# Reordering the projections, chains, first loads and output norm of a hybrid decoder layer

## The chip, the cores and the metric

The kernel runs on one core of one Trainium2 chip. The core has five engines with a queue of instructions each: TensorE (PE, matrix products), VectorE (DVE), ScalarE (ACT), GpSimd (POOL) and SyncE (SP, here used to issue DMAs). Each works through its queue in order, and semaphores tie them together. The metric is the time of one execution on the device in microseconds (us), lower is better; of several runs the median is taken.

## The reference

One decoder layer on 256 tokens of width 2048, all in float32:

```
u = rmsnorm(x, norm_mix_w)
q_a, k_a, v_a, z_a, beta_a, dec_a, q_b, k_b, v_b, gate_a, gate_b = split(u @ w_in)
y_a = gated_deltanet(...)      # causal conv of 4 taps + silu, l2 norm of q and k, chunked delta rule
                               # (a triangular solve per chunk), then rmsnorm(o) * silu(z_a)
y_b = moba_attention(...)      # 8 heads of 128, rmsnorm of q and k, relative bias, softmax
mix = sigmoid(gate_a) * (y_a @ w_branch_gdn) + sigmoid(gate_b) * (y_b @ w_branch_moba)
h   = x + mix @ w_out
u   = rmsnorm(h, norm_ffn_w)
out = h + (silu(u @ w_ffn_gate) * (u @ w_ffn_up)) @ w_ffn_down
```

The two branches have 8 heads of 128 each; the feed-forward width is 5632. With 256 tokens the attention has one block, so each query attends to its own past only.

## The kernel before

**Matrix products.** Each float32 product is made of three (or, where one matmul covers two, fewer instructions) products of rounded parts: a weight unit of 128 x 1024 values is loaded (`wraw`, seven buffers, issued by SP), ACT rounds it to `whi`, DVE subtracts to get `wlo` (L64, L65, four buffers each), and PE multiplies both with the upper and lower part of the activations. `Weights.get(u)` issues loads six units ahead and splits three units ahead. There are 504 units, in the order in which the jobs take them.

**Jobs.** `fm_jobs` (L143) makes a result with channels on partitions: per unit 8 pairs of a 512-wide (L156) and a 256-wide matmul (L157). `tm_job` (L165) makes one with tokens on partitions: per unit 12 matmuls of 512 (L177 to L179). The convolution's q, k, v projections are fm jobs of 4 units; z, attention's q, k, v, the gates, the branches and all later products are tm jobs.

**Chains.** The small work (norms, DeltaNet, attention) is written as Python generators in the list `chains`. `tick()` is called after every second unit (TICK): it first runs what is in `late` (convolution taps; `turn`, the transposes of a result), then one step, a hop, of the first chain. The framework's scheduler then puts each engine's instructions in order, by program order and by when it expects their inputs.

**Order of the work.** Group 0's convolution jobs (x is scaled and split beside the first two), beta and decay, z of group 0, then group 1's convolution jobs with `gdn(0)` running in the ticks beside them, z of group 1, attention's projections of both groups with the chains behind, gate and branch jobs of the first branch (`yaT`), of the second (`ybT`), w_out, feed-forward, down projection. A convolution job is evicted by ACT and DVE (L262, L263), scaled (L340), gets six taps of DVE (L348) and a silu (L350, L351).

**Inside `gdn`.** Decay matrices (L396 to L400, the subtraction on POOL), transposes and squares for the norms of q and k (L410, L412), the scaled products (`decayed`, L428), a pass through DRAM for the 16 x 16 blocks (`dm`, `lb`, L451 to L454), fifteen dependent steps of DVE (L470, L471), the solve of the two token halves, one after the other, each in one hop (L496 to L546), and `solve`, `attend` and `finish`. `finish` squares on ACT, takes a reciprocal root by twelve small DVE operations (`rsqrt`), multiplies twice on POOL (L569, L570), and transposes into yaT (L574).

**Inside `moba`.** Norm of q and k, transposes (L643), then per pair of heads the load of the bias (L653, SP), scores (L658 to L660), softmax (L662 to L673) and the product with v (L681 to L688).

**First loads.** SP loads `wmix` and W0 in two halves, then W1 to W6; ACT queues all of x's transposed chunks (L199, L202). `x_part` (L211) splits the unit first, then makes four pieces of aT, upper part on ACT (L215), lower on DVE (L216).

## Time and profile before

| | us |
|---|---|
| median of 3 runs (1499.58 to 1500.82) | 1499.75 |
| the profiled execution | 1498.37 |
| its span, first to last instruction | 1496.6 |
| PE busy | 1474.1 (98%) |
| DVE busy | 868.9 (58%) |
| ACT busy | 675.8 (45%) |
| POOL busy | 56.7 (4%) |

Busy time is the union of an engine's instructions. Matmuls are pipelined, so one that takes 390 ns from start to end is followed by the next after some 225 ns; the distance between starts tells the rate. An engine's idle time is put down to the instruction that released it. The granted TensorE clock is shown as 1.00 over the whole span.

### The profile page before, as it was taken

Reading aid. Unit: us, or ns where it says so; the run is one execution under the profiler, and the core shown is the slowest. Engines: PE = TensorE matmul, PEld = TensorE weight load, DVE = VectorE, ACT = ScalarE, POOL = GpSimd, SP = SyncE. Lnnn points to the kernel's source line nnn. Section 1 sums busy time; section 2 is a strip of 40 time slices with the busy share of each in tenths; the row PEclk is TensorE's granted clock in tenths of the full one; section 3 lists DMA queues with packets and bytes.
Section 4 is the critical chain, followed back from the end, with each engine's and each line's share of the span. In section 5 each row is a group of like instructions: output and inputs, shape, how many; then the busy total and the mean of one; then the engine's idle time right before and its main releaser. Section 6 shows DMA issues by size and latency. Waiting matters only on the chain.

```text
span 1496.6 us, 18724 instructions
## 1 busy us (share of the span) xinstructions
PE 1474.1 (98%) x7164; PEld 1227.0 (82%) x7164; DVE 868.9 (58%) x1161; ACT 675.8 (45%) x956; POOL 56.7 (4%) x48
## 2 busy tenths in 40 slices
PE   7999999999999999999999999999999999999998
PEld 6888778887878888888888888888888888888887
DVE  5978957866664445555565555555555555444443
ACT  6645445445454444444554444444444444333332
POOL 0003002301100000000000000000000000000000
PEclk9999999999999999999999999999999999999999
DMA  9564744753546666667666666666666566666661
GB/s 372 168 189 127 209 124 142 191 177 115 181 127 199 195 195 184 187 193 241 192 184 186 194 186 194 184 192 187 196 185 193 186 186 194 194 206 207 194 210 58
DMA packets 77450, 277.82 MB, mean 186 GB/s; under 512 B 8752, under 2 KB 9392, under 8 KB 76976
## 3 DMA queue, kind: packets, MB, share of 16 engines
q1 hardware_dynamic: 75456, 270.46, 59.7%
q10 hardware_dynamic: 1424, 4.59, 1.2%
q0 software_dynamic: 480, 1.57, 0.3%
q8 instruction: 56, 0.92, 0.3%
q14 instruction: 34, 0.28, 0.1%
HBM read 274.36 MB, written 2.23 MB: 185 GB/s over the span
## 4 chain that ended last, share of the span: by engine, by line
PE 91%; DVE 4%; DMA 2%; ACT 1%; issue 1%; POOL 0%; SPq 0%; DVEq 0%; ACTq 0%; POOLq 0%
PE ps L179 27%; PE ps L177 27%; PE ps L178 27%; PE ps L156 3%; PE ps L157 2%; PE pT L189 1%; DVE wlo L65 1%; DMA lb<-dm 1%; DMA bias<-in_relt 1%; DVE cacc L348 1%; DMA wraw<-in_w 0%; ACT whi L64 0%; PE pU L551 0%; PE pO L559 0%; PE pb L279 0%
## 5 line engine op out<-in xcount | busy, mean ns | idle before, releaser
L65 DVE TENSOR_TENSOR wlo<-wraw,whi 128x1024 fp32r<-128x1024 f32 (+1 forms) x505 | 619.9, 1229 | 521.7 <-ACT whi L64 519.7
L64 ACT CAST whi<-wraw 128x1024 fp32r<-128x1024 f32 (+1 forms) x505 | 530.0, 1051 | 680.2 <-PE ps L179 608.0
L177 PE MATMUL ps<-whi,uT 128*128 128x512 f32 x704 | 274.8, 390 | 0.0
L179 PE MATMUL ps<-whi,uT 128*128 128x512 f32 x704 | 273.9, 389 | 0.0
L178 PE MATMUL ps<-wlo,uT 128*128 128x512 f32 x704 | 273.9, 389 | 0.0
L177 PE MATMUL ps<-whi,aT 128*128 128x512 f32 x512 | 202.8, 396 | 0.0
L179 PE MATMUL ps<-whi,aT 128*128 128x512 f32 x512 | 201.3, 393 | 0.0
L178 PE MATMUL ps<-wlo,aT 128*128 128x512 f32 x512 | 200.4, 391 | 0.0
L179 PEld LDWEIGHTS ps<-whi,uT 128*128 128x128 f32 x704 | 132.2, 188 | 27.5
L177 PEld LDWEIGHTS ps<-whi,uT 128*128 128x128 f32 x704 | 132.2, 188 | 27.0
L178 PEld LDWEIGHTS ps<-wlo,uT 128*128 128x128 f32 x704 | 132.2, 188 | 27.0
L156 PE MATMUL ps<-aT,whi 128*128 128x512 f32 x384 | 137.6, 401 | 10.3 <-DVE aT L216 10.2
L179 PEld LDWEIGHTS ps<-whi,aT 128*128 128x128 f32 x512 | 96.2, 188 | 19.7
L177 PE MATMUL ps<-whi,high 128*128 128x512 f32 x288 | 112.0, 389 | 0.0
L178 PE MATMUL ps<-wlo,high 128*128 128x512 f32 x288 | 112.0, 389 | 0.0
L179 PE MATMUL ps<-whi,high 128*128 128x512 f32 x288 | 112.0, 389 | 0.0
L157 PE MATMUL ps<-aT,wlo 128*128 128x256 f32 x384 | 108.6, 283 | 3.1 <-DVE wlo L65 3.1
L178 PEld LDWEIGHTS ps<-wlo,aT 128*128 128x128 f32 x512 | 96.3, 188 | 18.7
L177 PEld LDWEIGHTS ps<-whi,aT 128*128 128x128 f32 x512 | 96.3, 188 | 18.4
L156 PEld LDWEIGHTS ps<-aT,whi 128*128 128x128 f32 x384 | 73.0, 190 | 27.4 <-DVE aT L216 10.2
L157 PEld LDWEIGHTS ps<-aT,wlo 128*128 128x128 f32 x384 | 73.4, 191 | 4.1 <-DVE wlo L65 4.0
L178 PEld LDWEIGHTS ps<-wlo,high 128*128 128x128 f32 x288 | 54.1, 188 | 11.3
(327 smaller groups left out, 1394.3 us busy)
## 6 DMA issues: line engine op xcount, KB each, us to landing
wraw<-in_w SPq DMA_DIRECT2D x503, 512.0 KB, 4.0
xrow<-in_xtok SPq DMA_DIRECT2D x1, 2048.0 KB, 10.2
lb<-dm ACTq DMA_DIRECT2D x2, 1024.0 KB
xr<-in_xtok SPq DMA_DIRECT2D x8, 256.0 KB, 5.5
xc<-in_xT ACTq DMA_DIRECT2D x3, 512.0 KB, 8.1
out<-fo POOLq DMA_DIRECT2D x6, 256.0 KB, 4.4
bias<-in_relt SPq DMA_DIRECT2D x4, 256.0 KB, 4.1
xc<-in_xT ACTq DMA_DIRECT2D x2, 256.0 KB, 5.0
```

Source lines behind the costliest of these rows:

```text
L64: self.last_hi = self.nc.scalar.copy(hi[:, f], raw[:, f])
L65: self.last_lo = self.nc.vector.tensor_sub(lo[:, f], raw[:, f], hi[:, f].bitcast(F32))
L156: nc.tensor.matmul(ps[:, j], hi[:, sl], act[:, kc], start=kc == 0, stop=False)
L157: nc.tensor.matmul(ps[:, j, :T], lo[:, sl], act[:, kc, :T], start=False, stop=kc == nk - 1)
L177: nc.tensor.matmul(ps[:, n], ah, hi[:, sl], start=kc == 0, stop=False)
L178: nc.tensor.matmul(ps[:, n], ah, lo[:, sl], start=False, stop=False)
L179: nc.tensor.matmul(ps[:, n], al, hi[:, sl], start=False, stop=kc == nk - 1)
L189: nc.tensor.transpose(p[:, i], src[:, i * P:(i + 1) * P], ident)
L348: nc.vector.scalar_tensor_tensor(acc[:, j, d:], u[:, j, :T - d], w[:, 3 - d:4 - d], acc[:, j, d:], op0=ALU.mult, op1=ALU.add)
```

## The change

It does the following.

- The projections of a head group come in the order convolution, z, attention; `gdn(g)` starts before z, and `moba(g)` follows it in the list of chains. Two gate jobs of the first branch come ahead of its first branch job.
- `tick()` is called after every unit instead of every second. The chains are cut into shorter hops, with `rest(n)` for empty ones; the solve treats both token halves in each hop, and the fifteen steps are spread over five hops. The bias of a pair of heads is loaded ahead.
- First loads: ACT issues only the two halves of x's first chunk, SP the halves of W0 and then W1, x chunk 1, W2, W3, x chunk 2, W4, W5, x chunk 3, W6. The first unit is split by halves between the pieces of aT, and its matmuls go by k. Nine matmuls on a tile of ones stand at the head of PE's queue.
- The output norm is four scalar_tensor_tensor per half on DVE instead of two multiplications on POOL; two more POOL operations (L593, L604) go to DVE, and the decay's subtraction becomes the bias of four exponentials on ACT.
- In the last down projection the last four k steps go by token half, into PSUM tiles of their own.

The diff, cut to its core:

```diff
-TICK = 8
+WARM = 9
...
-    def load(self, u, cuts=1):
-        if u in self.raw or u >= self.n:
+    def load(self, u, f=slice(0, 1024)):
+        if u >= self.n or (u in self.raw and f.start == 0):
             return
-        t = self.raw[u] = self.pool.tile([P, 1024], F32, name="wraw", tag="wraw", bufs=RAW)
-        for i in range(cuts):
-            f = slice(i * 1024 // cuts, (i + 1) * 1024 // cuts)
-            self.nc.sync.dma_start(t[:, f], self.src[u, :, f])
-
-    def split(self, u):
+        if f.start == 0:
+            self.raw[u] = self.pool.tile([P, 1024], F32, name="wraw", tag="wraw", bufs=RAW)
+        self.nc.sync.dma_start(self.raw[u][:, f], self.src[u, :, f])
+
+    def split(self, u, by_parts=False):
         if u in self.parts or u >= self.n:
             return
         self.load(u)
         raw = self.raw[u]
         hi = self.pool.tile([P, 1024], F32R, name="whi", tag="whi", bufs=4)
         lo = self.pool.tile([P, 1024], F32R, name="wlo", tag="wlo", bufs=4)
-        for f in (slice(0, 512), slice(512, 1024)) if u == 0 else (slice(0, 1024),):
+        self.parts[u] = (hi, lo)
+
+        def part(f):
             self.last_hi = self.nc.scalar.copy(hi[:, f], raw[:, f])
             self.last_lo = self.nc.vector.tensor_sub(lo[:, f], raw[:, f], hi[:, f].bitcast(F32))
-        self.parts[u] = (hi, lo)
+
+        if by_parts:
+            return part
+        part(slice(0, 1024))
...
+    def rest(n):
+        for _ in range(n):
+            yield
...
-                for j in range(2):
-                    for kc in range(k0, k0 + 4):
-                        sl = slice((kc % 4) * 256 + j * P, (kc % 4) * 256 + (j + 1) * P)
-                        nc.tensor.matmul(ps[:, j], hi[:, sl], act[:, kc], start=kc == 0, stop=False)
-                        nc.tensor.matmul(ps[:, j, :T], lo[:, sl], act[:, kc, :T], start=False, stop=kc == nk - 1)
-            if k0 % TICK == TICK - 4:
-                tick()
+                order = [(j, kc) for j in range(2) for kc in range(k0, k0 + 4)]
+                if cursor[0] == 1:
+                    order.sort(key=lambda jk: jk[1])
+                for j, kc in order:
+                    sl = slice((kc % 4) * 256 + j * P, (kc % 4) * 256 + (j + 1) * P)
+                    nc.tensor.matmul(ps[:, j], hi[:, sl], act[:, kc], start=kc == 0, stop=False)
+                    nc.tensor.matmul(ps[:, j, :T], lo[:, sl], act[:, kc, :T], start=False, stop=kc == nk - 1)
+            tick()
...
-    def tm_job(act, nk):
+    def tm_job(act, nk, last=0):
 
         get = act if callable(act) else lambda kc: act[:, kc]
-        ps = mm.tile([P, NT, 512], F32, name="ps", tag="mm")
-        for kc in range(nk):
-            if kc % 2 == 0:
-                hi, lo = W.get(cursor[0])
+        if last:
+            ps = [aux.tile([P, 512], F32, name="ps", tag="aux") for _ in range(NT)]
+        else:
+            both = mm.tile([P, NT, 512], F32, name="ps", tag="mm")
+            ps = [both[:, n] for n in range(NT)]
+        order = [(kc, n) for kc in range(nk - last) for n in range(NT)]
+        order += [(kc, n) for n in range(NT) for kc in range(nk - last, nk)]
+        units = {}
+        for kc, n in order:
+            if kc // 2 not in units:
+                units[kc // 2] = W.get(cursor[0])
                 cursor[0] += 1
+            hi, lo = units[kc // 2]
             sl = slice((kc % 2) * 512, (kc % 2) * 512 + 512)
-            for n in range(NT):
-                ah = get(kc)[:, n * P:(n + 1) * P]
-                al = get(kc)[:, T + n * P:T + (n + 1) * P]
-                nc.tensor.matmul(ps[:, n], ah, hi[:, sl], start=kc == 0, stop=False)
-                nc.tensor.matmul(ps[:, n], ah, lo[:, sl], start=False, stop=False)
-                nc.tensor.matmul(ps[:, n], al, hi[:, sl], start=False, stop=kc == nk - 1)
-            if kc % (TICK // 2) == TICK // 2 - 1:
+            ah = get(kc)[:, n * P:(n + 1) * P]
+            al = get(kc)[:, T + n * P:T + (n + 1) * P]
+            nc.tensor.matmul(ps[n], ah, hi[:, sl], start=kc == 0, stop=False)
+            nc.tensor.matmul(ps[n], ah, lo[:, sl], start=False, stop=False)
+            nc.tensor.matmul(ps[n], al, hi[:, sl], start=False, stop=kc == nk - 1)
+            if n == NT - 1 and kc % 2 == 1:
...
-        W.load(0, 2)
-        for c in range(1, KM // 4):
-            nc.scalar.dma_start(xcs[c], xT[:, 4 * c:4 * c + 4])
+            W.load(0, slice(512 * i, 512 * i + 512))
         for u in range(1, RAW):
             W.load(u)
-            if u == 4:
-                nc.sync.dma_start(ident, consts[:, :P])
-                nc.sync.dma_start(par, params)
+            if u % 2:
+                c = u // 2 + 1
+                nc.sync.dma_start(xcs[c], xT[:, 4 * c:4 * c + 4])
+        nc.sync.dma_start(ident, consts[:, :P])
+        nc.sync.dma_start(par, params)
         warm = small("warm", [2])
         nc.scalar.activation(warm, ones[:, :2], AF.Tanh)
+        busy = aux.tile([P, 512], F32, name="busy", tag="aux")
+        for _ in range(WARM):
+            nc.tensor.matmul(busy[:, :P], ones, ones, start=True, stop=True)
 
         def x_part(k0):
-            W.split(cursor[0])
+            part = W.split(cursor[0], k0 == 0)
             for k in range(4):
+                if part and k % 2 == 0:
+                    part(slice(256 * k, 256 * k + 512))
...
-            nc.gpsimd.tensor_sub(d, d, bc(gc[:, n, hs], P))
-            nc.scalar.activation(d, d, AF.Exp)
+            for h in range(GH):
+                nc.scalar.activation(d[:, h], d[:, h], AF.Exp, bias=ngc[:, n, g * GH + h:g * GH + h + 1])
             dec.append(d)
+            yield
         junk = t2("junk")
...
+            if n == 0:
+                yield
             tmp = t2("mtmp")
             nc.vector.tensor_mul(tmp, m, bcm(mneg, GH))
             nc.vector.tensor_reduce(mc[:, n * GH:(n + 1) * GH], tmp.rearrange("p h (b i) -> p h i b", i=BS),
                                     axis=AX.X, op=ALU.add)
-            if n == 0:
-                yield
+            yield
...
+        for i in range(1, BS):
+            with tc.issue_after(W.last_lo.ins):
+                if i == 1:
+                    nc.vector.tensor_copy(X, bcm(eye, NT * GH))
+                nc.vector.tensor_mul(prod[:, :, :i + 1], lbv[:, :, i, :i + 1], X[:, :, :i + 1])
+                nc.vector.tensor_reduce(X[:, :, i], prod[:, :, :i + 1], axis=AX.X, op=ALU.add)
+            if i % 3 == 0:
+                yield
...
+        E, D, Y = [], [], []
+        wide = [P, GH, P // BS, BS]
+        for n in range(NT):
             e = t2("E")
-            wide = [P, GH, P // BS, BS]
             nc.vector.tensor_mul(e.rearrange("p h (b i) -> p h b i", i=BS),
                                  X[:, n * GH:(n + 1) * GH].unsqueeze(2).to_broadcast(wide),
                                  mblk.rearrange("p (b i) -> p b i", i=BS).unsqueeze(1).to_broadcast(wide))
+            E.append(e)
...
+            D.append(t2("D"))
+            nc.scalar.copy(D[n], p)
+        yield
...
+        def finish(os):
+            ros = []
+            for n, o in enumerate(os):
+                ss = small(f"os{g}{n}", [GH])
+                junk = t2("junk")
+                for h in range(GH):
+                    nc.scalar.activation(junk[:, h], o[:, h], AF.Square, accum_out=ss[:, h:h + 1])
+                ros.append(ss)
+            yield
+            for n, o in enumerate(os):
+                ro = rsqrt(f"or{g}{n}", ros[n], 1.0 / DH)
+                for h in range(GH):
+                    nc.vector.scalar_tensor_tensor(o[:, h], o[:, h], ro[:, h:h + 1], zw[:, n, h],
+                                                   op0=ALU.mult, op1=ALU.mult)
+                yield
...
-        nc.gpsimd.tensor_sub(rr1, vs[1], rr1)
+        nc.vector.tensor_sub(rr1, vs[1], rr1)
...
+        erq = small(f"erq{g}", [GH])
+        nc.vector.tensor_mul(erq, eg1[:, hs], rq[:, 1])
+        nc.vector.tensor_mul(o1, p, bc(erq, P))
+        yield
         vn1 = solve(1, rr1)
+        yield
         p = attend(1, vn1)
-        nc.vector.tensor_add(o1, p, o1)
-        nc.gpsimd.tensor_mul(o1, o1, bc(rq[:, 1], P))
-        yield
-        yield from finish(1, o1)
+        for h in range(GH):
+            nc.vector.scalar_tensor_tensor(o1[:, h], p[:, h], rq[:, 1, h:h + 1], o1[:, h], op0=ALU.mult, op1=ALU.add)
+        yield
...
+        biases = []
+
+        def bias_load(h):
+            if h < GH:
+                biases.append(s2.tile([P, 2, T], F32, name="bias", tag="t2", bufs=14))
+                nc.sync.dma_start(biases[-1], relt[:, g * GH + h:g * GH + h + 2])
+
+        bias_load(0)
...
                 probs.append(s)
+                yield
+            bias_load(h + 2)
...
+    def ybt():
+        if not yb:
+            yb.append(acts.tile([P, H, 512], F32R, name="ybT", tag="actC"))
+        return yb[0]
+
     chains.append(beta_decay())
     for g in range(NG):
         qk, vT, zw = gdn_project(g)
         if g == 0:
             drain()
+        chains.append(gdn(g, qk, vT, zw))
         z_project(zw)
-        chains.append(gdn(g, qk, vT, zw))
-    for g in range(NG):
-        proj = moba_project(g)
-        if g == 0:
-            drain(1)
-            ybT = acts.tile([P, H, 512], F32R, name="ybT", tag="actC")
-        chains.append(moba(g, *proj, ybT))
+        chains.append(moba(g, *moba_project(g)))
...
-    mix = []
-    while len(chains) > NG:
-        tick()
+    mix, ahead = [], [gates(), gates()]
+    drain(1)
     for j in range(4):
-        mix.append([m for _, m in gated(yaT, "mix", lambda name: s2.tile([P, 512], F32, name=name, tag="t2", bufs=14))])
+        mix.append([m for _, m in gated(ahead.pop(0), yaT, "mix",
+                                        lambda name: s2.tile([P, 512], F32, name=name, tag="t2", bufs=14))])
+        if j < 2:
+            ahead.append(gates())
...
-        ps = tm_job(hid, KF)
+        ps = tm_job(hid, KF, 4 if j == 3 else 0)
...
     for g in range(NG):
         units += [m.reshape(-1, P, 1024) for m in a["by_group"][g]]
-        units.append(_tm(cut(a["z"], g)).reshape(-1, P, 1024))
-    for g in range(NG):
-        units += [_tm(cut(m, g)).reshape(-1, P, 1024) for m in a["qkv_b"]]
-    by_job = [(a["gates"][i], a["branches"][i]) for i in range(2)] + [(a["w_out"],), a["ffn"], (a["down"],)]
-    for ws in by_job:
+        units += [_tm(cut(m, g)).reshape(-1, P, 1024) for m in (a["z"],) + a["qkv_b"]]
+    gate, branch = _tm(a["gates"][0]), _tm(a["branches"][0])
+    units += [gate[0], gate[1], branch[0], gate[2], branch[1], gate[3], branch[2], branch[3]]
+    for ws in ((a["gates"][1], a["branches"][1]), (a["w_out"],), a["ffn"], (a["down"],)):
         units.append(np.concatenate([_tm(m) for m in ws], axis=1).reshape(-1, P, 1024))
```

## Rows read from the trace of the kernel before

**Rows 1.** The page: span, and each engine's busy time and instructions.

```profile
span 1496.6 us, 18724 instructions
...
PE 1474.1 (98%) x7164; PEld 1227.0 (82%) x7164; DVE 868.9 (58%) x1161; ACT 675.8 (45%) x956; POOL 56.7 (4%) x48
```

**Rows 2.** Waits of PE: waiting line, releaser: us in total, times, longest.

```profile
PE ps L156 <- DVE aT L216: 10.2, 1, 10.2
PE ps L157 <- DVE wlo L65: 3.1, 3, 1.5
PE pPT L681 <- DVE sc L672: 1.8, 2, 1.0
PE pD L504 <- DVE E L499: 1.8, 1, 1.8
PE pyT L574 <- POOL o L570: 0.8, 1, 0.8
```

**Rows 3.** Windows: stretch, its length, busy time (instructions) by engine, clock, DMA share, GB/s.

```profile
106.40:187.00 80.60, 75.78 (x453) 66.08 (x452) 72.21 (x136) 40.53 (x81) 13.25 (x9) 1.00 0.57 166
...
475.00:500.00 25.00, 25.00 (x112) 20.68 (x112) 11.66 (x11) 10.81 (x12) 0.00 (x0) 1.00 0.63 188
```

**Rows 4.** Timeline of the start: start, us, engine, line, operation, tiles, shape, count [idle before].

```profile
6.04 0.62 ACT L64 CAST whi<-wraw 128x512 fp32r<-128x512 f32 x1 [0.78 <-DMA wraw<-in_w]
...
8.41 0.62 ACT L64 CAST whi<-wraw 128x512 fp32r<-128x512 f32 x1 [1.75 <-DMA wraw<-in_w]
...
8.93 1.70 ACT L215 ACTIVATE aT<-xc,wmix 128x256 fp32r<-128x256 f32 x4
...
9.67 1.67 DVE L216 SCALAR_TENSOR_TENSOR aT<-xc,wmix,aT 128x256 fp32r<-128x256 f32 x4
...
11.01 0.63 PE L156 MATMUL ps<-aT,whi 128*128 128x512 f32 x1
...
11.64 0.63 PE L156 MATMUL ps<-aT,whi 128*128 128x512 f32 x1
...
14.64 0.40 PE L156 MATMUL ps<-aT,whi 128*128 128x512 f32 x1
...
14.99 0.39 PE L156 MATMUL ps<-aT,whi 128*128 128x512 f32 x1
```

**Rows 5.** Windows of two us at the start, columns as in rows 3.

```profile
2.00:4.00 2.00, 0.00 (x0) 0.00 (x0) 0.00 (x0) 0.24 (x1) 0.00 (x0) 1.00 0.86 229
...
4.00:6.00 2.00, 0.00 (x0) 0.00 (x0) 0.00 (x0) 1.25 (x2) 0.00 (x0) 1.00 0.95 316
```

**Rows 6.** Timeline of PE in the solve of group 0, first half.

```profile
193.05 0.43 PE L526 MATMUL pY<-D,mt 32*32 32x32 f32 x8
...
193.41 0.50 PE L179 MATMUL ps<-whi,aT 128*128 128x512 f32 x1
...
193.75 0.40 PE L177 MATMUL ps<-whi,aT 128*128 128x512 f32 x1
```

**Rows 7.** The load of xrow: timelines of SP and ACT; the page's DMA row.

```profile
22.78 0.42 SPq L220 DMA_DIRECT2D xrow<-in_xtok  x1
...
36.14 1.92 ACT L228 ACTIVATE xrow<-xrow 128x2048 f32<-128x2048 f32 x1
...
xrow<-in_xtok SPq DMA_DIRECT2D x1, 2048.0 KB, 10.2
```

**Rows 8.** DVE: timeline of the taps, one group of small operations, softmax tiles in a window.

```profile
50.52 4.03 DVE L348 SCALAR_TENSOR_TENSOR cacc<-cul,par,cacc 128x255 f32<-128x255 f32 x10
...
58.83 2.35 DVE L65 TENSOR_TENSOR wlo<-wraw,whi 128x1024 fp32r<-128x1024 f32 x2
...
L121 DVE TENSOR_TENSOR rr0w<-rr 128x16 f32<-128x16 f32 x3 | 0.5, 174 | 0.1
...
388.00:452.00 64.00, 4.36 (x24) 2.94 (x24) 14.03 (x48) 8.33 (x32) 1.00 0.48 144
```

**Rows 9.** Timeline of DVE at the end.

```profile
1492.07 1.29 DVE L822 TENSOR_TENSOR fo<-ps,h 128x512 f32<-128x512 f32 x2 [8.57 <-PE ps L179]
```

More of the change, by code (lines that the diff above doesn't have):

```diff
@@ L230, in x_scale @@
         nc.vector.tensor_scalar(r1h, r1, 0.5, None, op0=ALU.mult)
-        yield
+        yield from rest(2)
         p2 = aux.tile([P, 512], F32, name="pbc", tag="aux")
@@ L285, in beta_decay @@
             nc.tensor.transpose(pt[:, a * P:(a + 1) * P], sb[:, a], ident)
-        yield
+        yield from rest(2)
         bd = small("bd", [NT, 16])
@@ L334, in beta_decay @@
         nc.scalar.activation(eg1, gc[:, 1], AF.Exp)
-        bg.extend((beta, gc, egl, eg1))
+        ngc = small("ngc", [NT, H])
+        nc.vector.tensor_scalar(ngc, gc, -1.0, None, op0=ALU.mult)
+        bg.extend((beta, gc, ngc, egl, eg1))
     def conv(job, u, dst):
@@ L454, in gdn @@
         nc.scalar.dma_start(lb.rearrange("p j a i -> p (j a i)"), block.to_broadcast([P // BS, BS, BS * NT * GH * BS]))
-        yield
+        yield from rest(2)
         for n in range(NT):
@@ L587, in gdn @@
         nc.scalar.copy(S, p)
+        yield
         p = auxt("pkS")
@@ L597, in gdn @@
         o1 = t2("o")
-        nc.vector.tensor_mul(o1, p, bc(eg1[:, hs], P))
+        erq = small(f"erq{g}", [GH])
+        nc.vector.tensor_mul(erq, eg1[:, hs], rq[:, 1])
+        nc.vector.tensor_mul(o1, p, bc(erq, P))
         yield
-        yield from finish(0, o0)
         vn1 = solve(1, rr1)
+        yield
         p = attend(1, vn1)
-        nc.vector.tensor_add(o1, p, o1)
-        nc.gpsimd.tensor_mul(o1, o1, bc(rq[:, 1], P))
+        for h in range(GH):
+            nc.vector.scalar_tensor_tensor(o1[:, h], p[:, h], rq[:, 1, h:h + 1], o1[:, h], op0=ALU.mult, op1=ALU.add)
         yield
-        yield from finish(1, o1)
+        yield from finish((o0, o1))
     def moba_project(g):
@@ L625, in moba_project, with moba @@
         for n in range(NT):
-            nc.scalar.activation(vb[:, n], ps[:, n].rearrange("p (h d) -> p h d", h=GH), AF.Copy, scale=r1[:, n:n + 1])
+            nc.scalar.activation(vb[:, n], ps[n].rearrange("p (h d) -> p h d", h=GH), AF.Copy, scale=r1[:, n:n + 1])
         return ssb, raw, vb
-    def moba(g, ssb, raw, vb, ybT):
+    def moba(g, ssb, raw, vb):
         rb = rsqrt(f"rb{g}", ssb.rearrange("p w n h -> p (w n h)"), 1.0 / DH)
@@ L713, in gated @@
             s = mdt("gt")
-            nc.scalar.activation(s, pg[:, n], AF.Tanh, scale=r1h[:, n:n + 1])
+            nc.scalar.activation(s, pg[n], AF.Tanh, scale=r1h[:, n:n + 1])
             gate.append(s)
+        return gate
+    def gated(gate, yT, name, dst):
         pb = tm_job(yT, H)
@@ L741, in layer @@
     for j in range(4):
-        for n, m in gated(ybT, "mixb", mdt):
+        for n, m in gated(gates(), ybt(), "mixb", mdt):
             nc.vector.tensor_add(m, m, mix[j][n])
```

139 lines of the change are left out of this document (62 added, 77 removed).

## The prediction, made before the change was run

> **What bounds the kernel now.** I read the page first, then who TensorE waits for, then the windows, and only then the timeline. TensorE is busy 1474.1 of 1496.6 us [rows 1], so no other engine can be the bound over the whole. Its idle 22.5 us fall into three parts. The first 10.2 us wait for the first piece of aT; the waits behind that are 3.1 + 1.8 + 1.8 + 0.8 = 7.5 us [rows 2]; the last matmul ends with the sums of L822 at 1492.07 [rows 9], which leaves 4.5 us of tail. That is 22.2 of the 22.5.
>
> In a stretch of main matmuls only, 112 run in 25 us, one 512-wide matmul per 223 ns, while VectorE (DVE) is busy 11.66 and ScalarE (ACT) 10.81 of 25 us [rows 3]. Nothing waits there, and the whole kernel from 450 us on is such a stretch. A unit of weights (12 matmuls of 512, or 8 pairs of 512 + 256 in the convolution's projections) takes about 2.7 to 2.8 us. The number of main matmuls is the same after the change. What can be won lies in the first 450 us and in the tail.
>
> One stretch there is different: in 106.4 to 187 (the convolution projections of group 1, beside the DeltaNet chain of group 0) DVE is busy 72.21 of 80.6 us [rows 3], and the wait for wlo (3.1) and for E (1.8) fall in it: 4.9 us in which PE waits for DVE. Its other 8.4 us DVE stood idle in its own order.
>
> **The sum, part by part.**
>
> **First loads.** Today ACT queues the four x pieces beside SP's weights. The first half of W0 is split from 6.04 on; the second half only from 8.41, and since the split of both halves stands ahead of aT in ACT's order, aT begins at 8.93 and its lower part on DVE at 9.67 [rows 4]; the first matmul follows at 10.2 [rows 2]. After the change ACT issues only the first x chunk, W0's halves follow on SP, and later x chunks are woven into SP's row in order of need. At the rates of [rows 5] 2 x (229 + 316) kB = 1.09 MB have arrived at 6 us, which is x chunk 0 plus W0 (1.05 MB); I still let the first half come at 6.04, as now. Then half a split (0.62), aT's upper piece (1.70 / 4 = 0.43) on ACT, the half split (2.35 / 4 = 0.59) and aT's lower piece (1.67 / 4 = 0.42) on DVE [rows 4, 8]: 6.04 + 0.62 + 0.1 + 0.59 + 0.42 + 0.1 = 7.9. With the k-ordered first unit the first matmul needs only that. 10.2 - 7.9 = **-2.3 us**; between -1.0 (the pieces interleave badly on ACT) and -4.1 (the half arrives at 4.2, when half of these bytes have).
>
> **Nine warm matmuls.** The first pairs run 0.63 us apart, later ones 0.35 [rows 4]; 768 columns in 0.63 is the 1.2 GHz level, 0.35 the 2.4 GHz one, after about 4 us of matmuls. Six slow pairs cost 6 x 0.28 = 1.7 us. The nine run on `ones` long before the first load lands, so they cost nothing, and PE then sits idle again until 7.9. No row shows what an idle stretch does to the clock; the bounds are 0 and -1.7. I take **0**, today's state, and give the 1.7 to a rival. The Trainium skill (TensorE: Matmul & The Clock Gate, Part 1: The HAM clock gate) says the gate follows recent activity and an idle array drops back to its low level; by that rule the nine are worth nothing here, and the sum would stay as it is. No row here tests it.
>
> **Ticks at every unit, and the square of x.** SP issues the load of xrow at 22.78, it lands 10.2 us later at 33.0, and ACT squares from 36.14: 3.1 us spare [rows 7]. After the change the square comes a unit earlier (2.8) and everything 2.3 earlier, while the load stands behind the same bytes: ACT may sit up to 2.0 us. What covers it: a weight buffer comes free three units ahead of its use (four buffers), 8.3 us, of which the split takes 1.05 + 1.23 = 2.3; so ACT and DVE may fall behind by about 6 us. The row that shows it: DVE did eighteen taps and the pieces between from 50.52 to 58.83 without a split [rows 8], and no wait of PE lies there. If that cover is gone it costs the 2.0; I take **+0.5**. The later transposes (`turn`) also come one unit after their job instead of two: their source needs two or four DVE operations of about 0.65 [rows 9], 1.3 to 2.6 us, against a unit of 2.7. I take 0; if DVE begins with a split, the four moba mixes lose 1 us each at most.
>
> **Order of projections and single hops.** The chains now move one hop per unit. I count 38 hops for a DeltaNet chain and 17 for an attention chain. Group 0: z has 8 ticks and attention's projections 24, so 32 hops run where DVE has only splits and few evictions; the last six and the whole attention chain (16 more) take 22 of the 24 ticks of group 1's convolution. Group 1: 8 + 24 + 16 ticks (two gates ahead) cover the 38 hops and begin the attention chain, which ends inside the yaT jobs. So no drain runs bare. X's fifteen steps spread over five hops, eight units behind the load of lb as now, so I count nothing for them. The bias load moves forward on SP's queue; should its t2 slot not be free, weight loads stand behind it, and seven raw buffers (some four units ahead of the split) cover that. Removed: the wait on POOL for o (0.8), now none, because the norm is on DVE; the two waits for scores (1.8), since the bias load goes out at least three hops ahead and each head has its own hop. **-2.6 us**; between -1.2 and -3.8, as matmuls that wait less than these are not listed. POOL's subtraction for `dec` becomes the bias of four ACT exponentials; both lie off PE's path.
>
> Solving both halves in one hop also saves switching. A block of eight 32-wide matmuls starts at 193.05, the main matmul behind it at 193.41, the next at 193.75 [rows 6]: 0.70 for both, where eight cost about 8 x 0.03 and one main matmul 0.23, so some 0.25 to 0.3 per block. I count nine such blocks a group now, five after: 2 x 4 x 0.3 = **-2.4 us**, between 0 (the compiler keeps them apart) and -3.
>
> **The convolution of group 1** is where the change can pay back. DVE's work there after the change: 24 splits x 1.18 = 28.2; five jobs of six taps x 0.40 = 12.1; finals and evictions 16 to 17 pieces x 0.65 = 10.6 [rows 8, 9]; together 51. The hops that now land there: three reciprocal roots of twelve small operations at 0.17 to 0.2 = 6.5 [rows 8]; four heads at 14.03 / 8 = 7.0 [rows 8]; vn, yaT, q and k, ybT, rt: about 11 pieces x 0.6 = 6.6; and the new operations, three times four scalar_tensor_tensor of 128 x 128. No row has that shape with these operands: four cost between 0.65 (one 512-wide piece) and 1.6 (four 256-wide taps); I take 1.2, so 3.6. Sum 51 + 24 = 75, up to 78 with the high ends. PE needs 24 x 2.79 + 7.5 for the chains' matmuls = 74.5. The load on DVE is thus as tight as before (72.2 busy, 8.4 idle in order, 4.9 of stall). With three to six of in-order idling it is 0 to 9 over, and about 6 may be carried. PE's stall lies between 0 and 8; I take 4.0: **-0.9 us**.
>
> **Tail.** The two sums of L822 take 1.29 together and both start after the last matmul [rows 9]. With four k steps left over in n order, the first sum is done before the end: **-0.65**; between 0 and -0.7.
>
> Sum: -2.3 + 0 + 0.5 - 2.6 - 2.4 - 0.9 - 0.65 = **-8.4 us**. The profiled execution took 1498.37 (span 1496.6 and 1.8 around it), the median is 1499.75, 1.4 more. I take the difference off each: span 1488.2, execution 1490.0, median **1491.3 us**.
>
> **The rivals.** *A, DVE's lag is carried.* No wait of PE is left in group 1's convolution (-4.0) and the warm matmuls do lift the clock (-1.7): 1485.6. For it: z(1) behind the stage is light, so DVE can catch up there. Against it: today's stage stalls at 72 us of DVE work, less than I count.
>
> *B, the waits only move.* The 2.6 and 2.4 won come back as longer waits for wlo in that stage (4.9 + 1 instead of 4.0): 1491.3 + 5.0 + 1.9 = 1498.2, within 0.2% (3 us, about what a measurement of this kernel can tell from no change). For it: norm and attention join a stage that was already at 90% of DVE.
>
> *C, slower.* In group 1's convolution one hop stands one unit behind the other, and PE issues in order. Where a hop's matmuls read what DVE made in the hop before, and DVE has a split and some taps in front, PE waits as pD does now: 1.8 each [rows 2]. About twelve hops there are of that kind: 21.6 instead of 4.0, 1491.3 + 17.6 = 1508.9. It turns slower than before from 12.4 us of stall, seven such waits. Against it: main matmuls stand between the chain's in the trace, and 1.8 occurred once in twelve hops now.
>
> *D, the loads do not come sooner*, as all sixteen engines carry both rows of the queue anyway, and W0's halves still bound: the 2.3 is gone, 1493.6.
>
> **How the numbers follow.** Forecast 0.57, A 0.18, B 0.13, C 0.06, D 0.06. Faster by more than 0.2%: forecast, A, D = 0.81; within: B 0.13; slower: 0.06. The forecast's own terms span, at their ends, -18 to +3; the range goes from a little below A, 1483, to B, 1498.5, and leaves out C and the far end of A.
>
> **What would show it.** The first main matmul at 7.5 to 8.5; still 0.6 us between the first pairs; no wait of pyT or pPT in PE's list; waits for wlo of about 4 us within group 1's convolution and DVE above 90% busy there; a single sum behind the last matmul. Wrong would be: a wait of a microsecond at many hops, a first load later than 6 us, or a drain without main matmuls around it.

## The result and the profile after

The kernel before took 1499.68 us (median of four runs, 1499.58 to 1500.82), the changed one 1483.78 (1482.82 to 1485.74): ratio 0.9894, 95% interval 0.9877 to 0.9911. A second series gave 1499.17 and 1484.77, ratio 0.9903 (0.9889 to 0.9917). The forecast was 1491.3; the time lies at the low end of the range, nearest to rival A (1485.6). The profiled execution took 1483.21 us (before 1498.37), its span 1481.3 (before 1496.6), 15.3 less.

The page of the changed kernel, span and busy times, to be read beside [rows 1]:

```profile
span 1481.3 us, 18784 instructions
...
PE 1473.0 (99%) x7182; PEld 1230.7 (83%) x7182; DVE 867.4 (59%) x1188; ACT 677.8 (46%) x968; POOL 31.8 (2%) x32
```

DVE and ACT do as much as before, POOL 25 us less. The waits of PE in the changed kernel (columns as in [rows 2]):

```profile
PE ps L166 <- DVE aT L237: 1.9, 1, 1.9
PE busy L228 <- DVE ones L116: 1.1, 1, 1.1
PE ps L167 <- DVE wlo L66: 0.9, 1, 0.9
PE pb L300 <- DVE bw L297: 0.5, 1, 0.5
```

The four waits behind the first one in [rows 2] have gone: 3.1 for wlo in group 1's convolution, 1.8 for scores, 1.8 for E, 0.8 for POOL. The waits for wlo and bw in this list are new; both lie in group 0's convolution, at 61 and 70 us. Timeline of the start (columns as in [rows 4]):

```profile
1.06 4.21 PE L228 MATMUL busy<-ones 128*128 128x128 f32 x18 [1.06 <-DVE ones L116]
...
5.34 0.62 ACT L65 CAST whi<-wraw 128x512 fp32r<-128x512 f32 x1 [2.17 <-DMA wraw<-in_w]
...
6.60 0.88 DVE L237 SCALAR_TENSOR_TENSOR aT<-xc,wmix,aT 128x256 fp32r<-128x256 f32 x2
...
7.13 0.50 PE L166 MATMUL ps<-aT,whi 128*128 128x512 f32 x1 [1.86 <-DVE aT L237]
...
7.59 0.40 PE L166 MATMUL ps<-aT,whi 128*128 128x512 f32 x1
...
9.71 0.40 PE L166 MATMUL ps<-aT,whi 128*128 128x512 f32 x1
```

The first half of W0 is split at 5.34 instead of 6.04, the first main matmul runs at 7.13 instead of 10.2, and the pairs are 0.35 us apart from the second on (0.46 behind the first). 9.71 is the start of the eighth pair, 14.64 in [rows 4].

Group 1's convolution runs from 193.57 to 271.75 now. The window of that stage (columns as in [rows 3]):

```profile
193.57:271.75 78.18, 78.18 (x480) 69.41 (x479) 70.17 (x145) 44.24 (x84) 0.00 (x0) 1.00 0.52 160
```

PE is busy all of it. DVE is busy 70.17 us, 90%, the share it had in this stage before (72.21 of 80.6, [rows 3]). What differs is what DVE itself waits for. Its longest waits in the stage, in the kernel before:

```profile
DVE rr0x L117 <- ACT junk L412: 2.4, 1, 2.4
DVE k L415 <- ACT junk L412: 2.1, 1, 2.1
DVE prod L470 <- DMA lb<-dm: 2.0, 1, 2.0
```

and in the changed kernel:

```profile
DVE wlo L66 <- ACT whi L65: 3.7, 5, 2.5
DVE rhs L633 <- PE pkS L631: 2.7, 1, 2.7
DVE vn L586 <- PE pU L584: 1.3, 1, 1.3
```

Before, DVE stood in front of pieces of the chain, with splits queued behind them. In the two waits for `junk` ACT's casts stood still too: sixteen squares, from 113.6 to 120.5 us, were ahead of them in ACT's own queue. Now DVE's longest wait is for the split's own input, the cast `whi` that ACT makes. ACT in turn waits for PE to be done with a buffer, which it hardly did before; its waits of that kind in the stage, first in the kernel before, then in the changed one:

```profile
ACT whi L64 <- PE ps L156: 1.8, 1, 1.8
...
ACT whi L65 <- PE ps L166: 19.1, 13, 2.6
```

So the weights are ahead of PE there.

At the end one sum stands behind the last matmul, against two in [rows 9]; timeline of DVE:

```profile
1477.49 0.69 DVE L882 TENSOR_TENSOR fo<-ps,h 128x512 f32<-128x512 f32 x1 [2.03 <-PE ps L195]
```

### The profile page after: what moved, and what is told of

It is laid out like the page before. It is cut to its first block, busy times and chain, and to the rows that moved or that the text cites. A ratio compares the mean times of both kernels' runs of the same rounds, so it can differ in the third digit from the quotient of the medians.

```text
span 1481.3 us, 18784 instructions
## 1 busy us (share of the span) xinstructions
PE 1473.0 (99%) x7182; PEld 1230.7 (83%) x7182; DVE 867.4 (59%) x1188; ACT 677.8 (46%) x968; POOL 31.8 (2%) x32
## 4 chain that ended last, share of the span: by engine, by line
PE 97%; DVE 1%; issue 0%; DMA 0%; ACT 0%; POOL 0%; SPq 0%; DVEq 0%; ACTq 0%
PE ps L193 28%; PE ps L194 28%; PE ps L195 28%; PE ps L166 6%; PE ps L167 3%; PE pT L205 1%; PE pga L456 0%; DVE wlo L66 0%; DMA wraw<-in_w 0%; PE pb L300 0%; PE pX L541 0%; PE pY L534 0%; PE pU L584 0%; PE pO L592 0%; PE ptr L432 0%
## 5 line engine op out<-in xcount | busy, mean ns | idle before, releaser
L193 PEld LDWEIGHTS ps<-whi,high 128*128 128x128 f32 x288 | 54.1, 188 | 11.3
```

The lines of the kernel that those rows point to most:

```text
L193: nc.tensor.matmul(ps[n], ah, hi[:, sl], start=kc == 0, stop=False)
```

## The experiments

The times of a series carry about 2 us of uncertainty each, so that changes under 2 us are read from the profiles. The reference for them is the changed kernel at 1483.8 and 1484.8. In the profiled executions of the variants 1 to 3 us of the difference to the changed kernel's lie at the start, where the landing of the first load and the speed of the first matmuls change from execution to execution whatever the edit (table under **The start**).

**The order of the projections.**

```
         if g == 0:
             drain()
+        z_project(zw)
         chains.append(gdn(g, qk, vT, zw))
-        z_project(zw)
+    for g in range(NG):
         chains.append(moba(g, *moba_project(g)))
```

(and the units of weights in that order)

> The changed kernel with the projections in the order of before (convolution and z of group 0, convolution and z of group 1, then attention of both groups), the hops of the chains, a tick at every unit, the norm on VectorE and the rest kept. Theory O (the order takes the DeltaNet head of group 0, its POOL products and its serial small operations out of group 1's convolution): with the old order PE waits in group 1's convolution again, 4 to 6 us for wlo or E, the taps that run beside POOL take 1.26 us in place of 0.48, and the time is 1488 to 1490. Rival H (single hops and the spreading of the fifteen steps of X took the stall away): no wait of PE over 0.5 us in that stage and a time within 1.5 us of 1483.8.

Measured: 1490.79 us (1490.23 to 1491.74), ratio to before 0.9944 (0.9931 to 0.9956). By the times the order is worth 6 to 7 us of the 15. Of the 6.4 us by which the profiled span is longer, though, 1.2 to 1.8 lie at the start (first main matmul at 7.55, five slow pairs), so that about 5 are left for the order. PE's list has one large wait, `pD` for `E` with 3.2 us (`E` is the tile that the solve starts from, made out of X); the waits for wlo in that stage do not come back. PE's timeline at that place:

```profile
181.23 0.39 PE L194 MATMUL ps<-wlo,aT 128*128 128x512 f32 x1
184.80 1.25 PE L527 MATMUL pD<-ident,E 128*128 128x128 f32 x8 [3.18 <-DVE E L519]
185.81 0.48 PE L195 MATMUL ps<-whi,aT 128*128 128x512 f32 x1
186.22 3.65 PE L534 MATMUL pY<-D,ct 128*128 128x128 f32 x16
```

The sixteen matmuls of pY start 0.21 us apart where 0.11 is usual, 1.5 us lost on top of the wait. The window of that stretch shows a granted clock of 0.50, the 1.2 GHz level:

```profile
186.22:189.60 3.38, 3.38 (x17) 3.38 (x17) 1.67 (x3) 1.45 (x3) 0.00 (x0) 0.50 0.46 137
```

Why E is late stands in DVE's timelines: the first and the last step of X, with the old order,

```profile
159.92 0.18 DVE L510 TENSOR_TENSOR prod<-lb,X 128x16 f32<-128x16 f32 x1
...
183.72 0.29 DVE L511 TENSOR_REDUCE X<-prod 128x8 f32<-128x128 f32 x1
```

and in the changed kernel:

```profile
136.99 0.18 DVE L510 TENSOR_TENSOR prod<-lb,X 128x16 f32<-128x16 f32 x1 [4.09 <-DMA lb<-dm]
...
150.40 0.29 DVE L511 TENSOR_REDUCE X<-prod 128x8 f32<-128x128 f32 x1
```

The same thirty small operations take 24.1 us among the taps and splits of the convolution, and 13.7 beside the projections of z and attention. The part of theory O on the taps had no occasion: POOL's products ran from 131.4 to 140.9 us, and no tap ran between 126.8 and 143.1.

**The new order without the new hops**, in the kernel before:

```
-TICK = 8
+TICK = 4
...
+        chains.append(gdn(g, qk, vT, zw))
         z_project(zw)
-        chains.append(gdn(g, qk, vT, zw))
-    for g in range(NG):
-        proj = moba_project(g)
...
-        chains.append(moba(g, *proj, ybT))
+        chains.append(moba(g, *moba_project(g)))
```

> The kernel before with two edits: the projections in the new order (convolution, z and attention of group 0, then the same of group 1), and a tick at every unit, as the chains would not end otherwise; the long hops, the first loads, the norm on POOL and the tail stay as before. Theory O (the order is worth most of the gain): the 5.9 us of stalls around group 1's convolution go, the start and the tail stay, so about 1499.5 - 6 = 1493.5. Rival H (the order pays only with single hops, since a long hop a unit behind the one before makes PE wait in the middle of it): waits of 1 to 2 us at the hops of the solve, of the scores and of o, as many as before or more, 1498 or more.

Measured: 1532.98 us, ratio 1.0221 (1.0207 to 1.0235), 33.5 us slower than before. The largest waits of PE:

```profile
PE ps L178 <- DVE wlo L65: 19.8, 2, 10.0
...
PE pyT L574 <- POOL o L570: 9.1, 4, 2.4
PE pD L504 <- DVE E L499: 2.7, 2, 1.6
```

and what held DVE ahead of the first of the two waits for wlo:

```profile
130.24 0.18 DVE L470 TENSOR_TENSOR prod<-lb,X 128x16 f32<-128x16 f32 x1 [8.62 <-DMA lb<-dm]
130.34 1.22 DVE L65 TENSOR_TENSOR wlo<-wraw,whi 128x1024 fp32r<-128x1024 f32 x1
```

X's first step reached DVE 8.6 us ahead of its data, and the split behind it was needed. Four hops lie between the load of lb and X: eight units in the kernel before, four here, where a hop comes with every unit. In the changed kernel the products for `vs` were moved ahead of X and eight hops lie there; DVE still waits 4.09 us for lb, but PE does not stall behind it. So by the code these 19.8 us come from the ticks without the spacing rather than from the order; no rival of mine named them. The four waits for o, 2.1 to 2.4 us each, are rival C's mechanism at a little more than its 1.8. Rival H holds in so far as the order and the ticks lost time with the long hops; the order with the old ticks was not run. In group 1's convolution PE waits for nothing in this run either:

```profile
220.50:298.00 77.50, 77.43 (x456) 67.53 (x455) 60.99 (x103) 43.17 (x69) 0.00 (x0) 1.00 0.56 171
```

**More work on DVE, and on POOL, in group 1's convolution.**

```
         def taps():
+            if job >= 6:
+                for _ in range(2):
+                    nc.vector.tensor_mul(dst, u, u)
             acc = md.tile([P, 2, T], F32, name="cacc", tag="md", bufs=6)
```

(the other kernel the same on `nc.gpsimd`)

> The changed kernel with two more products of 128 x 512 on VectorE ahead of the taps of each of the six jobs of group 1's convolution (they write into the tile that ACT's tanh overwrites behind them): 12 x 0.6 = 7.2 us more of DVE there, 70.2 + 7.2 = 77.4 of a stage of 78.2 in which PE waits for nothing now. Theory S (what stalled PE in the kernel before was lateness of a serial chain, not DVE's sum; a lag of some microseconds is carried by the weight buffers): PE stalls at most 2 us, 1484 to 1486. Rival (the sum on DVE is the limit, as my prediction had it with 75 to 78 us and 4 us of stall): PE waits 4 us or more for wlo in that stage, 1488 or more.

> The same twelve products on POOL instead of VectorE, beside the taps, in the changed kernel. In the kernel before, four taps at 128 to 132 us took 1.26 us in place of 0.48, each beside a product of POOL of 1.1 us. Theory P (a product on POOL holds a scalar_tensor_tensor of VectorE up until it ends): some ten or more of the 36 taps take about 1.2 us, 8 to 12 us more on DVE in that stage, and PE stalls as much as with the load on VectorE or more: 1486 to 1492. Rival (the four long taps had another cause): all taps stay at 0.48 and the time is that of the changed kernel.

Measured: 1485.06 us with the load on VectorE, 1486.24 on POOL. The windows of the stage, changed kernel, VectorE, POOL:

```profile
193.00:272.00 79.00, 79.00 (x486) 70.19 (x485) 70.70 (x145) 45.02 (x86) 0.00 (x0) 1.00 0.52 161
```

```profile
193.00:272.00 79.00, 78.71 (x485) 69.70 (x484) 74.08 (x153) 45.26 (x86) 0.00 (x0) 1.00 0.50 153
```

```profile
193.00:272.00 79.00, 78.82 (x483) 69.67 (x483) 74.64 (x143) 43.70 (x85) 13.40 (x10) 1.00 0.52 159
```

Ten of the twelve products on VectorE fell into the window. DVE's busy time came to 74.1 us, 94% of the window, a little under the 75 to 78 that my prediction counted and above the 72.2 with which the kernel before stalled, and PE still idles only 0.3 of 79 us. DVE's sum is not what stalled PE. The longest and the median tap of group 1, POOL loaded (min/median/max in ns):

```profile
L372 DVE SCALAR_TENSOR_TENSOR cacc<-cul,par,cacc x36: 467/471/1260, 214.5 to 282.5; 128x255 f32<-128x255 f32 x12, 128x254 f32<-128x254 f32 x12, 128x253 f32<-128x253 f32 x12
```

Seven of the 36 were held, one to 0.82 us and six to about 1.26, five microseconds in all; without POOL's load none exceeds 0.49. Theory P holds in kind, with fewer taps than it named. The Trainium skill (SBUF — State Buffer, SBUF: two separate sides) says that a VectorE operation with two SBUF inputs and a GpSimd operation that reads SBUF exclude each other for a whole instruction; these taps agree. In the kernel before, POOL's products held four taps in the same way:

```profile
127.93 5.20 DVE L348 SCALAR_TENSOR_TENSOR cacc<-cul,par,cacc 128x255 f32<-128x255 f32 x5
...
128.16 1.15 POOL L430 TENSOR_TENSOR mt<-dec,bk 128x512 f32<-128x512 f32 x1 [11.65 <-DVE bk L423]
```

The 1 to 2 us on the time lie mostly at the start. The profiled spans are 1.9 and 2.9 us longer than the changed kernel's, and 1.5 and 1.7 of that are there before the stage begins (five slow pairs each). The rest is in short waits of PE: 0.3 for o with the load on VectorE, 0.2 for o and 0.4 for wlo with it on POOL.

**The start.** Without warm matmuls (`WARM = 0`), with four (`WARM = 4`), and with the loads of before:

```
-            W.load(0, slice(512 * i, 512 * i + 512))
+        for i in range(2):
+            W.load(0, slice(512 * i, 512 * i + 512))
+        for c in range(1, KM // 4):
+            nc.scalar.dma_start(xcs[c], xT[:, 4 * c:4 * c + 4])
...
-                if part and k % 2 == 0:
-                    part(slice(256 * k, 256 * k + 512))
+                if part and k == 0:
+                    part(slice(0, 512))
+                    part(slice(512, 1024))
...
-                if cursor[0] == 1:
-                    order.sort(key=lambda jk: jk[1])
```

> The changed kernel without its nine warm matmuls, nothing else. Theory W (the warm matmuls lift the clock, and the 1.9 us of idling behind them do not lose it): without them PE idles until 7.1, the first six or so pairs run 0.63 us apart as in the kernel before, and the time rises by 6 x 0.28 = 1.7 us, 1483.8 to about 1485.5. Rival (the clock came up early for another reason, or the first pairs wait for data in any case): the first pairs stay 0.35 apart and the time stays within 0.3 us. At 1485.5 both are within what the times alone can tell; the start of the seventh pair after the first decides (2.1 us behind it at 0.35, 3.8 at 0.63).

> The changed kernel with four warm matmuls in place of nine: eight passes of 0.213 us, so PE should be busy from 1.06 to about 2.8 and idle 4.3 us until 7.1. My prediction held that warm matmuls ahead of an idle stretch are worth nothing: then the first pairs are 0.63 apart and it costs 1.7 us against the changed kernel. Rival: any matmuls at the start keep their worth over the gap, pairs 0.35 apart and no change in time.

> The changed kernel with the first loads, the split of W0's two halves ahead of aT, and the order of the first unit's matmuls as before; nine warm matmuls and everything else kept. Theory (the order of loads is worth what the start shows): first main matmul at 10.2 in place of 7.1, so +3.1 us, 1486.9; if the longer idling of 5 us behind the warm matmuls loses the clock, 1.7 more, 1488.6. Rival (the later stages take the lag up, or the loads of before would have come sooner in this kernel anyway): less than +1 us.

Measured: 1485.72, 1484.87 and 1486.38 us. The changed kernel beside the later series:

> The changed kernel once more, beside the three that follow. Theory: its profile of 1483.2 us is not special, median 1483 to 1485. Rival (the first matmul at 7.13 and the clock kept over 1.86 us of idling were a lucky start; in the runs of its variants the first matmul came at 7.18 to 8.06 and five to seven pairs ran 0.63 apart): first matmul at 7.2 or later, some slow pairs behind it, and a median of 1484.5 to 1486.

1484.77 us. PE's timelines at the start, a row for each kernel (slow pairs: 0.6 us apart or more, where 0.35 is usual):

| kernel | warm matmuls end | first main matmul | slow pairs |
|---|---|---|---|
| before | none | 10.20 | first 6 |
| changed | 5.27 | 7.13 | none |
| changed, again | 5.27 | 7.16 | first 4 |
| no warm matmuls | none | 7.18 | first 9 |
| four warm | 3.14 | 7.73 | first 7 |
| old loads | 5.27 | 9.77 | first 6 |
| norm on POOL | 5.27 | 8.37 | first 8 |
| old order | 5.27 | 7.55 | 5, from the fourth on |
| plain tail | 5.27 | 8.06 | 5, from the fourth on |
| load on VectorE | 5.09 | 7.18 | 5, from the fourth on |
| load on POOL | 5.05 | 7.42 | 5, from the third on |
| halves apart | 5.27 | 7.21 | first 4 |

With the new loads the first main matmul comes at 7.13 to 8.37, always about 1.8 us behind the start of the first half split, which waits for its load to land (5.34 in the changed kernel, 6.58 with the norm on POOL); with the old ones at 9.77, 3.57 behind that split. So the loads are worth 1.4 to 2.6 us at the start, 1.8 for the same landing. Over the whole kernel the old loads cost less than the start shows: behind the slow pairs PE lies 4.3 us behind the changed kernel, at the end only 2.5. The waits for bw and wlo at 61 to 70 us do not occur with the old loads, though the ticks are the same; why, no run shows. Four warm matmuls leave PE idle for 4.6 us and seven slow pairs: for them my prediction's view holds. Nine leave none to eight, where nine run without any, and the idling behind them does not decide it alone: 1.86 and 1.89 us in the changed kernel's two executions, none and four slow pairs. Theory W is true of the changed kernel's first execution alone: of the eight executions in the table with nine warm matmuls and the new loads, the other seven have four to eight slow pairs. Two executions of the kernel without warm matmuls took 1490, three 1484.9 to 1485.7; the profiled one is of the longer kind. PE waits 1.7 us for E there, at 158 and 348 us, behind waits of DVE for lb of up to 5.7 us (4.1 in the changed kernel), and a wait for wlo of 1.87 us, which ends at 70.57, is followed by five slow pairs at a granted clock of 0.51:

```profile
71.14:74.28 3.14, 3.14 (x13) 2.66 (x12) 3.14 (x6) 0.22 (x1) 0.00 (x0) 0.51 0.78 227
```

**Three small parts**: the tail in plain order (`tm_job(hid, KF)`), the norm on POOL, the halves of the solve apart.

> The changed kernel with the last job in the plain order of steps, both sums of the output behind the last matmul as before. Theory: one sum more behind the last matmul, +0.65 us, and one 0.7 us tail stretch longer, 1484.5; the profile shows two sums after the last matmul. Rival: the write of the output ends last whichever sum is late, and the time stays within 0.2 us.

1485.75 us; the stretch behind the last matmul grows from 3.80 to 4.54 us, and two sums stand there. The theory holds in the profile (0.74); the time adds a late start (8.06, with five slow pairs).

```
-                for h in range(GH):
-                    nc.vector.scalar_tensor_tensor(o[:, h], o[:, h], ro[:, h:h + 1], zw[:, n, h],
-                                                   op0=ALU.mult, op1=ALU.mult)
+                nc.gpsimd.tensor_mul(o, o, bc(ro, P))
+                nc.gpsimd.tensor_mul(o, o, zw[:, n])
```

> The changed kernel with the output norm as two products on POOL, as before, in place of four scalar_tensor_tensor on VectorE; hops unchanged. Theory (in a hop of its own one unit of 2.7 us covers POOL's two products of 1.04 to 1.3 us, and DVE has room): PE waits at most 0.5 us for o, the time stays within 1 us of the changed kernel; taps beside POOL's products take 1.26 us. Rival (the norm on VectorE is what removed the wait, as my sum had it, with 0.8): waits of pyT for POOL of 0.8 to 2.5 us each at the four places, +2 to +6 us.

1485.01 us, and no wait for o in PE's list. With a hop of its own ahead of pyT the norm costs PE nothing on either engine; the profiled span is 2.7 us longer, and the late start with its eight slow pairs accounts for all of it. No tap ran beside POOL's products, so that the 1.26 had no occasion.

> The changed kernel with the two halves of the solve in hops of their own again from the 32-wide tiles on: four blocks more a group, each between main matmuls. My prediction put a block's switching at 0.25 to 0.3 us: +8 x 0.3 = 2.4 us. By the trace of the changed kernel (the first small matmul 0.12 late, the main matmul behind the block 0.20 late) it is 0.32 for each time PE goes from main matmuls to small tiles and back, so +2.6 us if the hops add eight of these. Rival (the blocks of one hop were apart already, since the scheduler puts main matmuls between them): within 0.5 us.

(Its edit: the `yield` behind each of the last four loops over the halves moves into the loop.) 1488.39 us, +3.6 against 1484.77 of its series; the profiled spans differ by 4.2. PE's timeline shows the size of one block, here in the changed kernel, where one hop's blocks were meant to lie together:

```profile
166.91 0.43 PE L554 MATMUL pY<-D,mt 32*32 32x32 f32 x8
167.27 0.50 PE L193 MATMUL ps<-whi,aT 128*128 128x512 f32 x1
167.60 0.39 PE L194 MATMUL ps<-wlo,aT 128*128 128x512 f32 x1
167.83 0.40 PE L195 MATMUL ps<-whi,aT 128*128 128x512 f32 x1
168.16 0.43 PE L554 MATMUL pY<-D,mt 32*32 32x32 f32 x8
168.52 0.50 PE L193 MATMUL ps<-whi,aT 128*128 128x512 f32 x1
```

The first small matmul comes 0.12 us late and the main one behind the block 0.20. Three main matmuls still stand between blocks of one hop. Summed over such delays the solve loses 4.5 us in the changed kernel of this series and 7.3 with the halves apart, 2.8 more: theory, not rival. The rest of the 4.2 lies in small delays that I did not trace.

**A version meant to be faster**: the first chunk and W0 in four pieces, twelve warm matmuls, and the operand of beta's matmuls prepared a hop ahead.

```
-        for i in range(2):
-            nc.scalar.dma_start(xcs[0][:, 2 * i:2 * i + 2], xT[:, 2 * i:2 * i + 2])
-            W.load(0, slice(512 * i, 512 * i + 512))
+        for i in range(4):
+            nc.scalar.dma_start(xcs[0][:, i:i + 1], xT[:, i:i + 1])
+            W.load(0, slice(256 * i, 256 * i + 256))
...
+        bw_part(0)
         for i in range(4):
+            bw_part(i + 1)
```

> A version made to be faster than the changed kernel. First: x's first chunk and W0 are loaded and split in four pieces each instead of two, so that the first matmul needs a quarter of W0 and one step of x; twelve warm matmuls in place of nine, so that PE idles less ahead of it. Second: the beta projection's operand is prepared one hop ahead, in buffers of the solve's pool, so that its matmuls do not wait for VectorE (0.5 us) and DVE does not wait for a buffer. Theory: first main matmul at 6.2 to 6.6 in place of 7.1, pairs 0.35 apart throughout, no wait of pb: -1 to -1.5 us, and the waits of wlo at 70 us (0.9) may go as well. Rival (the landing of the loads sets the pace of the first unit, not its first piece): the first matmul is earlier but pairs stall behind it, and the time stays within 0.5 us of the changed kernel.

1484.16 us, against 1484.77 of its series: no difference. The first main matmul comes at 5.89, but the first pieces stall behind one another, and the waits only change place:

```profile
PE ps L167 <- DVE wlo L66: 1.3, 2, 0.8
...
PE ps L194 <- DVE wlo L66: 1.0, 1, 1.0
PE ps L166 <- DVE aT L237: 0.3, 1, 0.3
```

## Why the prediction was too cautious

The direction and the place of the gain were right; the sizes were not. For each term I took the microseconds that PE's matmuls lie beyond the usual distance of their kind, before less after, in the two profiled executions:

| term of the sum (us) | predicted | measured |
|---|---|---|
| first loads | -2.3 | -3.1 |
| nine warm matmuls | 0 | -1.6 |
| ticks at every unit, square of x | +0.5 | +2.4 |
| order and single hops (waits of o, scores, pr) | -2.6 | -4.5 |
| switching in the solve | -2.4 | -1.6 |
| convolution of group 1, with E behind it | -0.9 | -5.9 |
| tail | -0.65 | -0.75 |
| sum | -8.4 | -15.1 |

The span shrank by 15.3; the rest of 0.2 is in delays too short to list.

**The convolution of group 1** is the step that failed. I counted DVE's work after the change (75 to 78 us), set it against PE's 74.5, and took 4.0 us of stall. The count was near (70.2), the limit was not. "Today's stage stalls at 72 us of DVE work, less than I count" took DVE's sum for the cause. The added products brought DVE to 74.1 of 79 us, and PE idled 0.3. Before, the stalls were 0.6 + 1.7 + 1.6 us for wlo and 2.0 for E (as distances of starts, so a little more than the waits in [rows 2]), and 6.5 of the 8.4 us that I called idle "in its own order" were DVE's waits for ACT and for lb, with splits queued behind. With the old order in the changed kernel the waits for wlo stay away and E is 3.2 us late. So the order is what E needed, once the hops are spaced: X's serial steps run beside work that is light on DVE. The waits for wlo went without the order, and in the kernel before they leave this stage with the new order and the old hops too, since the head of the chain, with its waits for ACT and lb, then runs elsewhere (and stalls PE there). Which part of the change removes them with the old order (the extra gates, POOL's products made earlier, the spread of X) I did not separate; the four taps that POOL held took 3.1 us more of DVE's time just ahead of the first two of these stalls. Rival A had the outcome, no wait of PE in that stage, and I gave it 0.18. Its reason, a lag of DVE that is carried, is not what the trace shows: ACT waits 19.1 us for PE to free buffers, so DVE does not lag.

**First loads**: the mechanism was as told. The first half of W0 was split at 5.34 where I kept 6.04, and 7.9 less 0.7 is 7.2, against the 7.13 measured; in other executions it landed later, up to 6.58.

**Nine warm matmuls**: they were not over "long before the first load lands" but at 5.27, as each fp32 one runs as two passes of 0.21 us, and PE idled 1.9 us. My value of 0 and rival A's 1.7 are both seen in executions, and mine is nearer to most of them: the kernel before has six slow pairs, seven of the eight executions have four to eight. The -1.6 of the table is one lucky start. The rule of the Trainium skill that I weighed there (TensorE: Matmul & The Clock Gate, Part 1: The HAM clock gate) does not settle it; the same section says that the number of slow matmuls at the start varies from run to run of one kernel, and the table above agrees: none and four.

**Ticks at every unit**: the place was wrong. The square of x waits for nothing: the load of xrow lands at 32.0, ACT begins at 33.8. The 2.4 us arise at 61 to 70 us, where beta's hops, now a unit apart, fall among the taps of three jobs: pb waits 0.5 for bw, and the split behind them is 0.9 late. The ticks alone don't make these waits: with the old loads and the same ticks there are none, and in the kernel before with a tick at every unit there is one, of 1.4 for wlo. That the 2.4 belongs to this term is therefore not shown.

**Switching**: 0.3 a block was right. The count was wrong, "nine such blocks a group now, five after": PE's order keeps main matmuls between the blocks of one hop, and the main matmuls behind blocks lose as much as before (2.9 against 2.7 us). What shrank are the delays of the chain's own tiles, 3.7 to 2.0 us.

**Order and single hops**: right in kind; the waits behind `pr`, too short to be listed, gave 1.0 more, and the listed 2.6 are 3.2 as distances. The reason for o was wrong: the hop took the wait away, the norm's engine didn't matter. **Tail**: right.

Of what I said would be seen, the waits for wlo of about 4 us in group 1's convolution did not come, and the slow first pairs came in some executions only; the first matmul came at 7.1, below the 7.5 that I named. No wait of pyT or pPT and the single last sum came as told; DVE was at 90%.

## What to carry to other kernels

An engine that is busy 90% of a stage need not be what stalls it: look at what it waits for itself, and whether urgent work is queued behind that wait; a test is to add work to it and see whether the bound engine moves. Serial chains of small operations belong beside the projections whose operands need little of the same engine, and a hop must not reach an engine before its data, or everything behind it waits too. A reordering and the spacing of its steps are one change: the new order with a tick at every unit and the long hops cost 33.5 us here; with the steps spaced the order gave some 5 to 7.

## What the runs showed of the hardware that I had not expected

- A stall can be paid twice. PE waited 3.18 us for E, ran 1.4 us, and then ran 3.4 us at a granted clock of 0.50; after 1.87 us for wlo and 0.6 us of matmuls, 3.1 us at 0.51. Behind the two stalls of 10 us in the new order without the new hops stand 4.4 and 6.0 us at 0.50. The stalls of the kernel before, 1.5 to 2.0 us, show no such stretch.
- The first half of W0, 0.26 MB queued first, landed between 5.3 and 6.6 us in executions with the same loads, and the first matmul moved with it.
- At the start the granted clock's column says 1.00 in executions whose pairs are 0.64 us apart (the changed kernel again, 7.16 to 9.88). There only the distance of the matmuls shows the level.
- In four of the kernels with nine warm matmuls the first two or three pairs ran 0.35 to 0.47 us apart and the next five at 0.60 to 0.65, while PE was busy without a break.
- A product on POOL held a tap of VectorE from 0.48 to 1.26 us: four times in the kernel before (128 to 132 us), six times in full with the load on POOL. Beside POOL's memsets, in the changed kernel at 54 to 57 us, the taps kept 0.47 to 0.48.
